# Two pairs of early loads merged into one transfer each, and gamma split in 8 pieces, in a streaming RMSNorm + GELU kernel

## The chip, the cores and the metric

The kernel runs on one core of one Trainium2 chip. The metric is the time of one execution on the device in microseconds (us). "Engines" without a name are compute engines (ACT is ScalarE, DVE is VectorE, POOL is GpSimd, SP is SyncE); the 16 engines that move data are always called DMA engines here. All runs named below gave correct results. All were in the normal ("fast") state, with one exception that is marked.

## The reference

For `x` of shape 8 x 1024 x 2048 (fp32, 67.1 MB) and `gamma` of 2048 values:

```python
rms = np.sqrt(np.mean(x ** 2, axis=-1, keepdims=True) + eps)
out = gamma * x / rms
return 0.5 * out * (1 + np.tanh(np.sqrt(2 / np.pi) * (out + 0.044715 * out ** 3)))
```

Every element is read once and written once, so 134.25 MB cross between HBM and SBUF. That is the work that the time is spent on.

## The kernel before

The 8192 rows are cut into 16 groups of 4 MB (128 partitions x 4 rows x 2048). Six slots in SBUF hold a group each. Loads are issued by SyncE and stores by ScalarE, so there are two DMA queues. In a pass over the groups ScalarE does the squares of group `g`, POOL makes the reciprocal root, DVE multiplies by gamma, and ScalarE then does the GELU of group `g - 1` and issues its store. The load that reuses the slot follows it.

```python
    slot = [sbuf.tile([P, R, D], FP32, name=f"slot{i}") for i in range(SLOTS)]
    ...
    store_pieces = {G - 1: [(0, 2), (2, 2)]}      # the last group is stored in two parts
    ...
    def load(g):
        nc.sync.dma_start(out=slot[g % SLOTS], in_=x3[g])
    ...
    def gelu_store(g):
        for r, n in store_pieces.get(g, [(0, R)]):
            ...                                    # GELU of the rows r .. r+n, in place
            nc.scalar.dma_start(
                out=o3[g, :, r : r + n, :], in_=slot[g % SLOTS][:, r : r + n, :]
            )
    ...
        for g in range(SLOTS):
            load(g)
        nc.scalar.dma_start(                       # gamma, in D // GW = 16 pieces
            out=gamma_row[:, :, 0:GW],
            in_=gamma.rearrange("(o a b) -> o a b", o=1, b=GW),
        )
        ...
        for g in range(G + 1):
            if g < G:
                squares(g)
                inverse_rms(g)
                scale(g)
            if g:
                gelu_store(g - 1)
                if g - 1 + SLOTS < G:
                    load(g - 1 + SLOTS)
```

Completion of a transfer is told by a semaphore; the transfers of the program take eight of them in turn. At the end SyncE waits for all of them, in a fixed order, before the program closes.

Of the kernel before, what the change touches and what calls it, by code (L numbers as in the profile page):

```python
# [1 line left out]

# [4 lines left out]

FP32 = mybir.dt.float32
ALU = mybir.AluOpType
ACT = mybir.ActivationFunctionType  # L10

P = 128
ROWS = 4
SLOTS = 6

GW = 128


@with_exitstack
def kernel(  # L20
    ctx: ExitStack,
    tc: tile.TileContext,
    x: bass.AP,
    gamma: bass.AP,
    eps: bass.AP,
    out: bass.AP,
):




    nc = tc.nc
    D = x.shape[-1]
    R = ROWS
    eps_f = float(eps)
    x3 = x.rearrange("b s d -> (b s) d").rearrange("(g p r) d -> g p r d", p=P, r=R)
    o3 = out.rearrange("b s d -> (b s) d").rearrange("(g p r) d -> g p r d", p=P, r=R)
    G = x3.shape[0]

    sbuf = ctx.enter_context(tc.tile_pool(name="sbuf", bufs=1))  # L40
    psum = ctx.enter_context(
        tc.tile_pool(name="psum", bufs=1, space=bass.MemoryType.PSUM)
    )
    slot = [sbuf.tile([P, R, D], FP32, name=f"slot{i}") for i in range(SLOTS)]
    gamma_row = sbuf.tile([1, D // GW, GW + 16], FP32, name="gamma_row")
    ones = sbuf.tile([1, P], FP32, name="ones")
    warm = sbuf.tile([1, 1], FP32, name="warm")
    power = sbuf.tile([P, R], FP32, name="power")
    ssq = sbuf.tile([P, G, R], FP32, name="ssq")
    rstd = sbuf.tile([P, G, R], FP32, name="rstd")  # L50
    ms = sbuf.tile([P, R], FP32, name="ms")
    y = sbuf.tile([P, R], FP32, name="y")
    z = sbuf.tile([P, R], FP32, name="z")
    gamma_ps = psum.tile([P, D], FP32, name="gamma_ps")
    junk = psum.tile([P, D], FP32, name="junk")

    store_pieces = {G - 1: [(0, 2), (2, 2)]}
    scale_pieces = {G - 1: [(0, 1), (1, 1), (2, 1), (3, 1)]}

    def load(g):  # L60
        nc.sync.dma_start(out=slot[g % SLOTS], in_=x3[g])  # L61

    def squares(g):
        for r in range(R):
            nc.scalar.activation(  # L65
                out=junk,
                in_=slot[g % SLOTS][:, r, :],
                func=ACT.Square,
                accum_out=ssq[:, g, r : r + 1],
            )  # L70

    def scale(g):
        for r, n in scale_pieces.get(g, [(0, R)]):
            rows = slot[g % SLOTS][:, r : r + n, :]
            nc.vector.tensor_tensor(  # L75
                out=rows,
                in0=rows,
                in1=gamma_ps.unsqueeze(1).to_broadcast([P, n, D]),
                op=ALU.mult,
            )  # L80

    def inverse_rms(g):

        v = nc.gpsimd
        v.tensor_scalar(  # L85
            out=ms, in0=ssq[:, g, :], scalar1=1.0 / D, scalar2=eps_f,
            op0=ALU.mult, op1=ALU.add,
        )
        v.tensor_tensor(out=y, in0=ms, in1=power, op=ALU.pow)  # L89
        v.tensor_tensor(out=z, in0=y, in1=y, op=ALU.mult)  # L90
        v.tensor_tensor(out=z, in0=z, in1=ms, op=ALU.mult)  # L91
        v.tensor_scalar(  # L92
            out=z, in0=z, scalar1=-0.5, scalar2=1.5, op0=ALU.mult, op1=ALU.add
        )
        v.tensor_tensor(out=rstd[:, g, :], in0=z, in1=y, op=ALU.mult)  # L95

    def gelu_store(g):
        for r, n in store_pieces.get(g, [(0, R)]):
            for q in range(r, r + n):
                row = slot[g % SLOTS][:, q, :]  # L100
                nc.scalar.activation(  # L101
                    out=row, in_=row, func=ACT.Gelu_apprx_tanh,
                    scale=rstd[:, g, q : q + 1],
                )
            nc.scalar.dma_start(  # L105
                out=o3[g, :, r : r + n, :], in_=slot[g % SLOTS][:, r : r + n, :]
            )

    with tc.manual_schedule():
        for g in range(SLOTS):  # L110
            load(g)
        nc.scalar.dma_start(
            out=gamma_row[:, :, 0:GW],
            in_=gamma.rearrange("(o a b) -> o a b", o=1, b=GW),
        )
        nc.gpsimd.memset(power, -0.5)  # L116
        nc.vector.memset(warm, 0.0)  # L117
        nc.vector.memset(ones, 1.0)  # L118
        nc.scalar.activation(out=warm, in_=warm, func=ACT.Gelu_apprx_tanh)  # L119
        for k in range(0, D, 512):  # L120
            nc.tensor.matmul(  # L121
                out=gamma_ps[:, k : k + 512],
                lhsT=ones,
                rhs=gamma_row[:, k // GW : (k + 512) // GW, 0:GW],
                start=True,
                stop=True,
# [12 lines that stand above are left out]
# [1 line left out]
_INS = ['x', 'gamma', 'eps']  # L140
_OUTS = [((8, 1024, 2048), 'float32')]

_NUMBERS = {'eps': 9.999999747378752e-06}


# [26 lines left out]
```

## Time and profile before

| | before |
|---|---|
| time, median of 3 executions | 317.47 us (317.44 to 317.48) |
| the execution that was profiled | 318.66 us, of which the profile's span is 316.9 |
| transfers | 16 loads, 17 stores, 1 for gamma: 34 |
| DMA share of the span, by queue | loads 49.5%, stores 49.1% |
| ACT, DVE, POOL busy | 79%, 44%, 10% |

The lines below are from the page of the kernel before: the span, the busy tenths of ScalarE and of the DMA engines in 40 equal slices of it, the packets, the two queues (packets, MB, share of 16 DMA engines' span; q1 is the queue of the loads, q10 that of the stores), and the issues (KB each, median us from issue to landing).

```profile
span 316.9 us, 473 instructions
ACT  1379999999999997959689595995959859599800
DMA  8999999999999999999999999999999999999995
DMA packets 4787, 134.25 MB, mean 424 GB/s; under 512 B 544, under 2 KB 560, under 8 KB 560
q1 hardware_dynamic: 2304, 67.11, 49.5%
q10 hardware_dynamic: 2480, 67.12, 49.1%
slot<-in_x_dram SPq DMA_DIRECT2D x16, 4096.0 KB, 37.1
out_dram<-slot ACTq DMA_DIRECT2D x15, 4096.0 KB, 38.6
out_dram<-slot ACTq DMA_DIRECT2D x2, 2048.0 KB, 15.0
```

The DMA engines are at 9 tenths or more in all slices but the first and the last, while ScalarE pauses. The DMA engines bound this kernel. Of the 4787 packets 544 are under 512 bytes: these are the 4-byte writes that raise the semaphores, 34 transfers x 16 DMA engines. The Trainium skill says the same of the mechanism (page "DMA: Bandwidth & Descriptors", section "Why a DMA increments its semaphore by 16 and not by 1"): each DMA engine that takes part ends with a write of its own to the semaphore. The page's section "Specifications" gives 435 GB/s as the ceiling; the trace agrees, as a 32 KB packet takes 1.213 us, which is 432 GB/s for 16 DMA engines.

What SyncE waited for at the end of the kernel before (us in total, times, longest us). L167 is the closing of the program.

```profile
SPq L167 <- DMA out_dram<-slot: 39.6, 1, 39.6
SPq L167 <- DMA slot<-in_x_dram: 36.6, 1, 36.6
```

One long wait is for a load and one is for the last store. The trace has the times of what follows the last landing at 315.88 us: SyncE still goes through three more waits, long fulfilled, at 315.94, 316.00 and 316.06, then closes at 316.12. The end of the span is at 316.88, 1.00 us after the landing.

### The profile page before, as it was taken

How to read it: one execution, taken by the hardware profiler on the slowest of the kernel's cores; microseconds unless marked ns; L12 is line 12 of the kernel's file. 1: busy time of each engine (PE TensorE's matmuls, PEld its weight loads, DVE VectorE, ACT ScalarE, POOL GpSimd, SP SyncE). 2: the span in 40 equal slices, each digit the busy share in tenths (PEclk: the TensorE clock that was granted, in tenths of full speed). 3: DMA queues.
4: the chain of work that ended last, by engine and by line, in shares of the span. 5: the costliest groups of instructions: out<-in, count | busy, mean ns of one | idle time of the engine just before them, and what ended most of it. 6: DMA issues, size and time to landing. Idle time of an engine off the chain costs nothing.

```text
span 316.9 us, 473 instructions
## 1 busy us (share of the span) xinstructions
PE 7.2 (2%) x8; PEld 2.5 (1%) x8; DVE 139.4 (44%) x21; ACT 251.1 (79%) x194; POOL 32.3 (10%) x101
## 2 busy tenths in 40 slices
PE   0900000000000000000000000000000000000000
PEld 0300000000000000000000000000000000000000
DVE  0038909090919191732808246091550905582000
ACT  1379999999999997959689595995959859599800
POOL 0020102020202020202002020020200102001000
DMA  8999999999999999999999999999999999999995
GB/s 328 414 451 426 434 393 459 401 459 402 459 405 455 426 434 431 430 434 426 438 426 455 410 455 418 443 426 430 434 430 435 422 459 405 459 414 447 422 420 230
DMA packets 4787, 134.25 MB, mean 424 GB/s; under 512 B 544, under 2 KB 560, under 8 KB 560
## 3 DMA queue, kind: packets, MB, share of 16 engines
q1 hardware_dynamic: 2304, 67.11, 49.5%
q10 hardware_dynamic: 2480, 67.12, 49.1%
q14 instruction: 3, 0.02, 0.0%
HBM read 67.12 MB, written 67.11 MB: 424 GB/s over the span
## 4 chain that ended last, share of the span: by engine, by line
DMA 56%; ACT 33%; issue 5%; ACTq 1%; SPq 0%
DMA slot<-in_x_dram 30%; DMA out_dram<-slot 26%; ACT slot L101 19%; ACT junk L65 14%; ACTq L105 1%; SPq L61 0%; ACTq L101 0%; ACTq L65 0%
## 5 line engine op out<-in xcount | busy, mean ns | idle before, releaser
L75 DVE TENSOR_TENSOR slot<-slot,gamma_ps 128x8192 f32<-128x8192 f32 (+1 forms) x19 | 139.2, 7340 | 147.0 <-ACT junk L65 147.0
L65 ACT ACTIVATE junk<-slot 128x2048 f32<-128x2048 f32 x64 | 120.4, 1881 | 47.3 <-DMA slot<-in_x_dram 43.7
L101 ACT ACTIVATE slot<-slot,rstd 128x2048 f32<-128x2048 f32 x64 | 122.8, 1989 | 0.9 <-ACT slot L101 0.9
L85 POOL TENSOR_SCALAR ms<-ssq 128x4 f32<-128x4 f32 x16 | 3.1, 194 | 247.5 <-ACT junk L65 247.5
L89 POOL TENSOR_TENSOR y<-ms,power 128x4 f32<-128x4 f32 x16 | 16.1, 1009 | 1.3
L65 ACT ACTIVATION_READ_ACCUMULATOR junk<-slot 128x1 f32 x64 | 12.0, 188 | 0.0
L121 PE MATMUL gamma_ps<-gamma_row,ones 1*128 1x512 f32 x8 | 7.2, 1072 | 8.4 <-DMA gamma_row<-in_gamma_dram 8.4
L95 POOL TENSOR_TENSOR rstd<-z,y 128x4 f32<-128x4 f32 x16 | 3.2, 201 | 1.3
L91 POOL TENSOR_TENSOR z<-z,ms 128x4 f32<-128x4 f32 x16 | 3.2, 201 | 1.3
L90 POOL TENSOR_TENSOR z<-y 128x4 f32<-128x4 f32 x16 | 3.2, 199 | 1.3
L92 POOL TENSOR_SCALAR z<-z 128x4 f32<-128x4 f32 x16 | 3.1, 194 | 1.4
L121 PEld LDWEIGHTS gamma_ps<-gamma_row,ones 1*128 1x128 f32 x8 | 2.5, 325 | 11.5 <-issue 11.5
L119 ACT ACT_TABLE_LOAD x1 | 1.3, 1283 | 1.3 <-PEq L153 1.3
L117 DVE MEMSET warm<- 1x1 f32 x1 | 0.1, 59 | 0.8 <-PEq L153 0.8
L119 ACT ACTIVATE warm<-warm 1x1 f32<-1x1 f32 x1 | 0.2, 202 | 0.0
L118 DVE MEMSET ones<- 1x128 f32 x1 | 0.2, 165 | 0.0
L116 POOL MEMSET power<- 128x4 f32 x1 | 0.1, 102 | 0.3 <-POOLq L153 0.3
L153 POOL MEMSET const-float32-0.0<- 128x1 f32 x1 | 0.1, 99 | 0.2 <-issue 0.2
L153 POOL MEMSET const-bfloat16-1.0<- 128x1 bf16 x1 | 0.1, 102 | 0.0
L153 POOL MEMSET const-uint8-127<- 128x1 uint8 x1 | 0.1, 102 | 0.0
L153 POOL MEMSET const-float32-1.0<- 128x1 f32 x1 | 0.1, 99 | 0.0
## 6 DMA issues: line engine op xcount, KB each, us to landing
slot<-in_x_dram SPq DMA_DIRECT2D x16, 4096.0 KB, 37.1
out_dram<-slot ACTq DMA_DIRECT2D x15, 4096.0 KB, 38.6
out_dram<-slot ACTq DMA_DIRECT2D x2, 2048.0 KB, 15.0
gamma_row<-in_gamma_dram ACTq DMA_DIRECT2D x1, 8.0 KB, 7.5
```

The lines of the kernel that those rows point to most:

```text
L65: nc.scalar.activation(out=junk, in_=slot[g % SLOTS][:, r, :], func=ACT.Square, accum_out=ssq[:, g, r : r + 1],)
L75: nc.vector.tensor_tensor(out=rows, in0=rows, in1=gamma_ps.unsqueeze(1).to_broadcast([P, n, D]), op=ALU.mult,)
L85: v.tensor_scalar(out=ms, in0=ssq[:, g, :], scalar1=1.0 / D, scalar2=eps_f, op0=ALU.mult, op1=ALU.add,)
L89: v.tensor_tensor(out=y, in0=ms, in1=power, op=ALU.pow)
L90: v.tensor_tensor(out=z, in0=y, in1=y, op=ALU.mult)
L91: v.tensor_tensor(out=z, in0=z, in1=ms, op=ALU.mult)
L92: v.tensor_scalar(out=z, in0=z, scalar1=-0.5, scalar2=1.5, op0=ALU.mult, op1=ALU.add)
L95: v.tensor_tensor(out=rstd[:, g, :], in0=z, in1=y, op=ALU.mult)
L101: nc.scalar.activation(out=row, in_=row, func=ACT.Gelu_apprx_tanh, scale=rstd[:, g, q : q + 1],)
L105: nc.scalar.dma_start(out=o3[g, :, r : r + n, :], in_=slot[g % SLOTS][:, r : r + n, :])
L119: nc.scalar.activation(out=warm, in_=warm, func=ACT.Gelu_apprx_tanh)
L121: nc.tensor.matmul(out=gamma_ps[:, k : k + 512], lhsT=ones, rhs=gamma_row[:, k // GW : (k + 512) // GW, 0:GW], start=True, stop=True,)
```

## The change

The intent is to remove those three waits from the end. With two transfers fewer, the last store gets another of the eight semaphores: the one that SyncE waits for last. So loads 2 and 3 become one transfer of 8 MB, and so do loads 4 and 5; for that, the six slots become parts of one tile. Gamma, which is read in pieces, is read in 8 pieces of 1 KB in place of 16 of 512 bytes.

```diff
-GW = 128
+GW = 256
+
+EARLY = [(0, 1), (1, 1), (2, 2), (4, 2)]
...
-    slot = [sbuf.tile([P, R, D], FP32, name=f"slot{i}") for i in range(SLOTS)]
+    ring = sbuf.tile([P, SLOTS, R, D], FP32, name="ring")
+    slot = [ring[:, i] for i in range(SLOTS)]
...
-    def load(g):
-        nc.sync.dma_start(out=slot[g % SLOTS], in_=x3[g])
+    def load(g, n=1):
+        i = g % SLOTS
+        nc.sync.dma_start(
+            out=ring[:, i : i + n], in_=x3[g : g + n].rearrange("g p r d -> p g r d")
+        )
...
-        for g in range(SLOTS):
-            load(g)
+        for g, n in EARLY:
+            load(g, n)
```

## The prediction

> **What bounds it now.** The 16 DMA engines. The profile's slices show DMA at 9 tenths or more in nearly every slice and a mean of 424 GB/s over the span; 2048 load packets and 1920 store packets of 32 KB take 1.21 us each, and all packets together take 312.2 us per engine of a 316.9 us span. That is at the 16-engine ceiling the Trainium skill gives ("DMA: Bandwidth & Descriptors", Specifications: about 435 GB/s). ACT is busy for 79%, DVE for 44%: both have slack. The trace begins moving data at 1.7 us; its last transfer lands at 315.88, its span ends at 316.88. In that last transfer 14 of 16 semaphore increments come by 313.83, the 15th at 314.89, the 16th at 315.88: two DMA engines lag.
>
> **What the change does.**
> 1. *End.* The semaphores of transfers rotate over eight. Before, the last store has number 1. SyncE ends with five wait instructions, over pairs (3,2), (4,1), (5,0), (6,PE), (7,ACT); the second one is released by the last store. Three more waits follow, one every 60 ns (315.94, 316.00, 316.06), then the drain at 316.12. With two transfers fewer (32 for 34), the last store gets number 7, the last of the five waits, so those three waits are over before. Saved: 3 x 60 ns = 0.18 us, all on the critical path, since nothing overlaps it. The rest of the closing barrier (0.75 us) stays.
> 2. *Two semaphore writes fewer per engine* (9 ns each in the packets) and gamma in 8 pieces instead of 16 (a 512-byte packet takes 27 ns; some engines lose one, others get one twice as long): under 0.05 us. Gamma is wanted by DVE at 21 us and its matmuls end at 15.5: off the path.
> 3. *Start.* Load 2 now lands with load 3 (42.2 us by the landings of before) and load 4 with load 5 (about 82). Before, the squares of group 2 began at 39.0, those of group 4 at 71.2. So ACT falls behind by about 3 us at group 2 and about 11 us at group 4: stores 1, 2 and 3 go out near 58, 74 and 98 us instead of 55, 71 and 87. The store queue holds 19.4 us of work per 4 MB store: store 2 ends at 102.7, so store 3 arrives 3 to 4 us before that, about as long as a store took from issue to its first packets (38.6 to 43.0). It may just run dry. ACT needs 16.1 us per group and the DMA 19.4, so 3.3 us per group are won back and by group 8 all is as before. Loads keep the engines busy in the meantime, so bytes are delayed, not lost. When the first store joined the loads, each engine had one packet about 0.5 us too long; if the store queue runs dry that may recur: up to +0.5 us, half likely.
> 4. *Which DMA engine ends last.* Its lag of 2 us over the others grew over the run (0.6 us spread at first, 3.4 at 259). Another order at the start may change it by up to 1 us either way. This is the largest uncertainty.
>
> **Prediction.** 317.47 - 0.18, with a little for step 3: 317.3 us, range 316.5 to 318.1. Faster by over 2%: 0.005; within 2%: 0.99; slower: 0.005.
>
> **Would show it right:** one wait instead of four between the last landing and the drain, and about 0.8 us from last landing to the end; ACT idle near 39 to 42 and 74 to 82 us; DMA still at 9 in all slices; total packet time unchanged.
>
> **Would show it wrong:** a slice near 100 us with DMA under 9; packets of the merged loads longer than 1.21 us; the last semaphore spread other than 2.6 us.

## More of the kernel before

The columns are the stretch and its length, the busy time of PE, PE's weight loads, DVE, ACT and POOL, the granted clock, the DMA share and GB/s.

```profile
180.00:200.00 20.00, 0.00 (x0) 0.00 (x0) 8.69 (x1) 16.24 (x14) 2.00 (x6) 1.00 1.01 434
200.00:220.00 20.00, 0.00 (x0) 0.00 (x0) 8.69 (x1) 16.21 (x15) 2.00 (x6) 1.00 1.00 433
220.00:240.00 20.00, 0.00 (x0) 0.00 (x0) 8.69 (x1) 16.22 (x13) 2.00 (x6) 1.00 1.00 431
240.00:260.00 20.00, 0.00 (x0) 0.00 (x0) 8.69 (x1) 15.52 (x13) 2.00 (x6) 1.00 1.00 433
```

The DMA share is 1.00 or 1.01 (a packet counts whole in the stretch in which it starts, so both columns vary a little), and 431 to 434 GB/s are moved.

## The result

| | before | after |
|---|---|---|
| time, median, same chip and rounds | 317.46 us (317.27 to 317.48, 4 executions) | 321.66 us (321.18 to 322.03, 4 executions) |
| span of the profile | 316.9 us | 319.4 us |
| last landing to the end of the span | 1.00 us | 0.84 us |

The ratio is 1.0133 (95%: 1.0115 to 1.0150). A ratio here is always the mean time of one kernel's fast runs over that of the other's of the same rounds, so not quite the ratio of the medians quoted. The kernel became 1.3% slower: under the 2% that would be called slower, but 3.6 us beyond the upper end of the predicted range. All outputs are right.

The page of the kernel after, the same lines:

```profile
span 319.4 us, 475 instructions
ACT  1379879992899999999999794985949859599800
DMA  8999999999999999999999999999999999999995
DMA packets 4739, 134.25 MB, mean 420 GB/s; under 512 B 504, under 2 KB 512, under 8 KB 512
q1 hardware_dynamic: 2272, 67.11, 49.9%
q10 hardware_dynamic: 2464, 67.12, 48.8%
out_dram<-ring ACTq DMA_DIRECT2D x15, 4096.0 KB, 34.7
ring<-in_x_dram SPq DMA_DIRECT2D x12, 4096.0 KB, 35.0
ring<-in_x_dram SPq DMA_DIRECT2D x2, 8192.0 KB, 59.5
```

The DMA line is the same to the digit. There are fewer packets (48 fewer), the same bytes, and yet the mean fell from 424 to 420 GB/s. The queues show where: q1 took 49.5% of 316.9 us, which is 156.9 us for each DMA engine, and now 49.9% of 319.4, which is 159.4: 2.5 us more. q10 took 155.6 and takes 155.9. The load packets became slower as a whole, though their number and size are the same; the store packets hardly did. The count of small packets agrees with the skill's rule for the number of DMA engines (same page, section "Why a DMA increments its semaphore by 16 and not by 1": at most 16, and such that it divides the slowest dimension): gamma in 8 pieces runs on 8 of them, and 31 x 16 + 8 is 504.

The windows view of the kernel after, the same stretches and columns:

```profile
180.00:200.00 20.00, 0.00 (x0) 0.00 (x0) 8.69 (x1) 15.66 (x13) 1.99 (x6) 1.00 1.00 421
200.00:220.00 20.00, 0.00 (x0) 0.00 (x0) 8.69 (x1) 15.68 (x13) 1.99 (x6) 1.00 1.01 426
220.00:240.00 20.00, 0.00 (x0) 0.00 (x0) 8.69 (x1) 15.88 (x13) 1.99 (x6) 1.00 1.00 423
240.00:260.00 20.00, 0.00 (x0) 0.00 (x0) 8.69 (x1) 15.51 (x13) 1.99 (x6) 1.00 0.99 418
```

The DMA share is still 0.99 to 1.01, at 418 to 426 GB/s for the 431 to 434 of before. So this is no idle time: it is busy time that moves less, 100 us and more after the merged loads have landed. These four stretches are the clearest: over the six stretches from 60 to 180 us the mean is 431 GB/s (before: 434).

The prediction's other steps hold. What SyncE waited for at the end, kernel after (L173 is the closing here):

```profile
SPq L173 <- DMA out_dram<-ring: 74.5, 5, 45.6
```

The last store's semaphore is now the last of the five. The trace has one wait after the last landing at 318.57 (at 318.584), and the closing at 318.65. From landing to closing that is 0.08 us for 0.24 before, and from landing to end 0.84 us are left of 1.00: 0.16 us were saved, where 0.18 were predicted. And the timeline of ScalarE in the kernel after (start us, us taken, instruction; in brackets the idle time before it and what ended it; cut to the store issues and the two long pauses):

```profile
38.37 0.36 ACTq L111 DMA_DIRECT2D out_dram<-ring  x1
...
42.19 1.88 ACT L71 ACTIVATE junk<-ring 128x2048 f32<-128x2048 f32 x1 [3.84 <-DMA ring<-in_x_dram]
...
57.89 0.34 ACTq L111 DMA_DIRECT2D out_dram<-ring  x1
...
73.97 0.34 ACTq L111 DMA_DIRECT2D out_dram<-ring  x1
...
80.76 1.88 ACT L71 ACTIVATE junk<-ring 128x2048 f32<-128x2048 f32 x1 [6.82 <-DMA ring<-in_x_dram]
...
96.46 0.34 ACTq L111 DMA_DIRECT2D out_dram<-ring  x1
```

Stores 1, 2 and 3 go out at 57.9, 74.0 and 96.5 us, where 58, 74 and 98 were predicted (before: 54.7, 70.8, 86.9). Store 3 is issued 5.3 us before store 2 lands (101.8, median over the DMA engines), so the store queue never ran dry.

### What the packets show

The trace records each packet with its start, duration, size and queue, but not its DMA engine. Chaining each packet to one that ends where it starts gives 16 chains, one for each DMA engine; a 4-byte write now and then falls into a neighbour's chain. Here is one chain of before and one of after around the first boundary between two stores. `L` is a load packet and `S` a store packet of 32 KB, with the start in us and the duration in ns; `L*` and `S*` are the semaphore writes that end a transfer on this DMA engine.

```
before  S@57.61:1213 L@58.82:1213 S@60.03:1213 L*@61.24:9 L@61.24:1213 S@62.45:1213 L@63.65:1213
        (its S*, at 61.24 too, stands in a neighbour's chain, which has two)
after   S@57.64:1213 L@58.85:1213 S@60.06:1213 L@61.27:1213 S*@62.48:9 L@62.48:1213 S@63.70:1213
```

Each DMA engine takes one packet of each queue in turn. That is what the Trainium skill says (page "DMA: Bandwidth & Descriptors", section "Queues, rings and completion order": a DMA engine goes round between its queues packet by packet, and SP and ACT own one ring each on all 16). A transfer of 4 MB is 8 packets and one semaphore write on each DMA engine. The chains show a thing that these sections leave out: **the semaphore write takes a turn of its own.** It lasts 9 ns, but in the kernel after, where the store queue spends its turn on `S*`, two load packets follow each other. Before, load and store boundaries coincide, both queues spend a turn on a semaphore write in the same round, and nothing shifts. The merged load of groups 4 and 5 has no semaphore write in its middle (at about 61 us). There the loads get ahead by one round, which is one load and one store packet, 2 x 1.213 = 2.43 us. And there they stay for the rest of the run:

| landing of, median of 16 DMA engines, us | in the middle of the run | store later than load by |
|---|---|---|
| before: loads | 100.4, 120.0, 139.3, 158.7 | |
| before: stores | 100.7, 120.2, 139.6, 158.9 | 0.2 |
| after: loads | 99.4, 118.9, 138.4, 158.0 | |
| after: stores | 101.8, 121.3, 140.8, 160.4 | 2.4 |

I call the last column the offset. At this offset of one round load packets become slow near the boundaries. One chain of after, and one of a later experiment (e13) in which the offset is three rounds:

```
after  L@174.22:1213 L@175.42:1213 L*@176.63:9 S@176.64:1371 L@178.01:1213 S*@179.22:9 S*@179.23:9
       L@179.24:1213 S@180.44:1213 L@181.65:1401 S@183.07:1220 L@184.28:1213
after  S@174.21:1213 S@175.43:1213 S@176.63:1213 L*@177.84:9 S@177.84:1213 L@179.05:1213 S*@180.26:9
       L@180.27:1934 S@182.20:1213 L@183.41:1215
e13    L*@174.01:9 S@174.01:1213 L@175.22:1213 S@176.43:1213 L@177.64:1213 S@178.85:1213 L@180.06:1213
       S*@181.27:9 L@181.28:1213 S@182.49:1213 L@183.70:1213
```

Counted over all chains: load packets longer than 1.3 us that start between 100 and 270 us are 9 before and 145 after. What all load packets take beyond 1.213 us, summed and divided by 16, is 1.51 us before (nearly all at the start, and near 41 us where the stores begin) and 4.15 us after: +2.64 us for each DMA engine, which is the +2.5 us of the queue line. While the merged loads themselves were in flight their packets were not slow.

For the traced execution of after (321.18) against the median one of before (317.47), 3.7 us are to be explained. The last store lands, on the median DMA engine, at 313.76 before and 316.49 after: +2.7 us, the slow load packets. The last DMA engine lags the median by 2.1 us in both traces; but the traced execution of before was itself 1.2 us over the median, and kernels that run at 317.4 (e6, e14) show a lag of only 0.8 to 0.9 us. So about +1.2 us is lag, an inference, as a median execution of before was not traced. The end gives -0.16.

In the trace of before, at least, the lag is no separate cause. One of the 16 chains has two stores and then two loads in a row at every boundary from 59.9 us on: this one DMA engine stands at the offset of one round, while the other 15 do not. It has 7 of the 9 slow load packets, and its load packets take 3.7 us beyond 1.213 each in sum, where those of the other chains take 1.0 to 2.0. That is about 2.3 us more than the middle chain (0.9 of it where the stores begin, 1.4 later), and the lag is 2.1. The traces of e6 and e14, at 317.4, have 2 slow load packets each. So the effect is seen inside one execution too, with 15 DMA engines as the comparison. What puts a single DMA engine there is not known.

### The profile page after: what moved, and what is told of

Its sections match the earlier page's. It is cut to its first block, busy times and chain, and to the rows that moved or that the text cites. A ratio compares the mean times of both kernels' runs of the same rounds, so it can differ in the third digit from the quotient of the medians.

```text
span 319.4 us, 475 instructions
## 1 busy us (share of the span) xinstructions
PE 7.2 (2%) x8; PEld 2.5 (1%) x8; DVE 139.4 (44%) x21; ACT 251.0 (79%) x194; POOL 32.1 (10%) x101
## 3 DMA queue, kind: packets, MB, share of 16 engines
q1 hardware_dynamic: 2272, 67.11, 49.9%
## 4 chain that ended last, share of the span: by engine, by line
DMA 60%; ACT 28%; issue 4%; another core or an unknown queue 2%; ACTq 1%; SPq 0%
DMA ring<-in_x_dram 35%; DMA out_dram<-ring 25%; ACT ring L107 17%; ACT junk L71 12%; ACTq L111 1%; SPq L65 0%; ACTq L107 0%
## 5 line engine op out<-in xcount | busy, mean ns | idle before, releaser
L81 DVE TENSOR_TENSOR ring<-ring,gamma_ps 128x8192 f32<-128x8192 f32 (+1 forms) x19 | 139.2, 7338 | 149.0 <-ACT junk L71 149.0
L71 ACT ACTIVATE junk<-ring 128x2048 f32<-128x2048 f32 x64 | 120.4, 1881 | 48.8 <-DMA ring<-in_x_dram 44.8
L107 ACT ACTIVATE ring<-ring,rstd 128x2048 f32<-128x2048 f32 x64 | 122.7, 1986 | 0.9 <-ACT ring L107 0.9
L71 ACT ACTIVATION_READ_ACCUMULATOR junk<-ring 128x1 f32 x64 | 11.9, 186 | 0.0
```

The costliest lines, as they stand in the source:

```text
L71: nc.scalar.activation(out=junk, in_=slot[g % SLOTS][:, r, :], func=ACT.Square, accum_out=ssq[:, g, r : r + 1],)
L81: nc.vector.tensor_tensor(out=rows, in0=rows, in1=gamma_ps.unsqueeze(1).to_broadcast([P, n, D]), op=ALU.mult,)
L107: nc.scalar.activation(out=row, in_=row, func=ACT.Gelu_apprx_tanh, scale=rstd[:, g, q : q + 1],)
```

## The experiments

Kernels of one batch ran on the same chip beside the kernel before. The batches are e1 to e4, e5 to e8, e9 to e12, e13 to e16, e17 and e18; the kernel before had medians of 317.43, 317.76, 317.39, 317.46 and 317.51 us in them.

The theories were: (offset) the missing turn of the load queue sets loads and stores apart, and the packets are slow because of that; (late) ScalarE's late groups 2 and 4, with late stores, are the cause; (merged) the 8 MB transfers, or the single tile, are the cause by themselves; (gamma) the 8 pieces are. All kernels are summed up in one table after the runs.

### e1: no merging, but the ring and gamma in 8 pieces

```diff
 (from after)
-EARLY = [(0, 1), (1, 1), (2, 2), (4, 2)]
+EARLY = [(0, 1), (1, 1), (2, 1), (3, 1), (4, 1), (5, 1)]
```

> The changed kernel without its merged loads: one ring tile and gamma in 8 pieces stay, six loads of 4 MB at the start. Theory 1 (turns: on each DMA engine the load queue and the store queue take turns packet by packet, and the 4-byte semaphore write that ends a transfer takes a whole turn; one load semaphore fewer while stores run puts the loads one packet ahead, so the ends of loads and stores no longer fall together, and the load packets beside a store's lone semaphore are slow): 317.4 us as before, excess of load packets over 1.21 us as before (1.6 us per DMA engine in the run). Theory 2 (ACT and so the stores are late): 317.4. Theory 3 (the new addresses of the ring, or gamma's share on 8 DMA engines, disturb the streams): 320 or more.

Measured: 318.52 us (317.27 to 319.13), ratio 1.0029 (1.0004 to 1.0055). Offset 0.2, 10 slow packets. The ring and gamma are not the main cause, though about 1 us stays with them.

### e2: only loads 2 and 3 merged; e3: only loads 4 and 5 merged

```diff
 (e2, from after; new line only)
+EARLY = [(0, 1), (1, 1), (2, 2), (4, 1), (5, 1)]
 (e3, from after; new line only)
+EARLY = [(0, 1), (1, 1), (2, 1), (3, 1), (4, 2)]
```

> Only loads 2 and 3 are one transfer (both end before the first store packet). Theory 1 (turns): no load semaphore is lost while stores run, so the ends of loads and stores stay together (medians within 0.3 us): 317.2 to 317.6. Theory 2 (late ACT): ACT is 3 us late for groups 2 to 4, so a part of the loss, 318 to 319. Theory 3 (a merged transfer is itself slow): half of the loss, 319 to 320.

> Only loads 4 and 5 are one transfer. Theory 1 (turns): one load semaphore is lost while stores run, loads end about 2.4 us before stores from then on: the whole loss, 321 to 322. Theory 2 (late ACT): most of the loss, about 320 to 321. Theory 3 (a merged transfer is itself slow): half, 319 to 320.

Measured: e2 319.21 us, ratio 1.0044 (1.0019 to 1.0069), offset 0.2, 24 slow packets. e3 321.98 us, ratio 1.0134 (1.0117 to 1.0151), offset 2.4, 139 slow packets. The merging of 4 and 5 carries it all; that of 2 and 3 does not, although it also is an 8 MB transfer. Turns tell them apart: the missing semaphore write of loads 2 and 3 falls at about 32 us, before any store runs (the first starts near 43 us), so there is no alternation to upset.

### e4 and e5: no merging, ScalarE made late on purpose

```diff
 (from before; e5. e4 had the same five squares, reading slot[g - 2])
             if g < G:
+                for r in range({2: 2, 4: 3}.get(g, 0)):
+                    nc.scalar.activation(
+                        out=junk, in_=slot[g][:, r, :], func=ACT.Square
+                    )
                 squares(g)
```

> The kernel before, with ACT made late by five extra squares with no use (two ahead of group 2, three ahead of group 4): stores 1, 2 and 3 go out near 58.8, 74.9 and 97.1 us, as in the changed kernel. No load is merged. Theory 1 (turns): 317.4 to 317.7, excess of load packets as before. Theory 2 (late ACT): 321 to 322, the whole loss.

> The run e4 waited for another group's load by mistake and is void for its question; this one repeats squares of the group that is next anyway. The kernel before, five extra squares without use on ACT (two ahead of group 2, three ahead of group 4): stores 1, 2, 3 near 58.8, 74.9 and 97 us, as in the changed kernel, no load merged. Theory 1 (turns): ends of loads and stores stay within 0.3 us of each other, 317.3 to 317.8. Theory 2 (late ACT): 320 to 322.

e4 was a mistake: the slot that its extra squares read had a new load under way, so they waited for it, ScalarE was late by some 60 us, and the DMA queues ran dry (372.3 us). It says nothing here. e5 puts stores 1, 2 and 3 at 58.6, 74.7 and 96.5 us, where the kernel after has 57.9, 74.0 and 96.5. Its four executions were 317.73, 321.05, 317.42 and 320.62 us, ratio 1.0038 (0.9979 to 1.0097). The traced one (317.73) has offset 0.3 and 9 slow packets. So lateness is not enough: two of four executions are as fast as before. But two are 3 us slower, and no trace of these exists. What they did stays open.

### e6 and e7: a tiny transfer added to one queue of the kernel before

A transfer of 64 bytes costs each DMA engine two turns of its queue (4 bytes of data, and the semaphore write), and next to no time. It is issued on ScalarE's queue after store 0 (e6), or on SyncE's before load 6 (e7).

```diff
 (e6, from before; e7 has nc.sync)
+    tiny = sbuf.tile([16, 1], FP32, name="tiny")
...
                 gelu_store(g - 1)
+                if g == 1:
+                    nc.scalar.dma_start(
+                        out=tiny, in_=gamma.rearrange("(a b) -> a b", a=16)[:, 0:1]
+                    )
```

> The kernel before with a transfer of 64 bytes without use (16 floats, one for each DMA engine) issued on ACT's queue right after store 0. Theory 1 (turns): its packet and its semaphore take two turns from the stores; counting turns, loads end 4 packets (4.9 us) ahead of stores from then on, and 64 bytes cost 2 us or more: 319.5 to 323. Theories 2 and 3: nothing is late or merged: 317.4.

> The kernel before with the same 64 bytes on SyncE's queue between loads 5 and 6. Theory 1 (turns): the loads lose two turns and end 2 packets (2.4 us) after the stores, the offset of the changed kernel with the other sign; every store's semaphore is again alone: 319 to 322 if only being apart counts, 317.4 if only loads ahead are harmful. Theories 2 and 3: 317.4.

Measured: e6 317.66 us, ratio 0.9990 (0.9966 to 1.0014), offset 4.9, 2 slow packets. e7 319.19 us, ratio 1.0041 (1.0012 to 1.0070), offset -2.5; between 80 and 100 us its packets took 1.1 us more than 1.213 each in sum, once, for each DMA engine (0.75 the loads, 0.36 the stores), and nearly nothing after. This supports one half of the theory and refutes the other as I first held it. Turns do set the offset, to the packet, with hardly a byte moved. But an offset as such costs nothing: at 4.9 us e6 has the speed of before. It must be the size of the offset.

### e8: the tiny transfer on SyncE's queue of the kernel after

```diff
 (from after, as e7)
+                    nc.sync.dma_start(
+                        out=tiny, in_=gamma.rearrange("(a b) -> a b", a=16)[:, 0:1]
+                    )
```

> The changed kernel with the same 64 bytes on SyncE's queue ahead of load 6. Theory 1 (turns): the loads lose two turns, which brings the ends of loads and stores together again (within 0.3 us): most of the loss comes back, 317.2 to 318.5, by adding a transfer. Theories 2 and 3: merged loads and late ACT stay, 321.5.

Measured: 342.8, 340.8, 343.46 and 317.19 us; the profiled one (342.8) counts as slow state, and no ratio is given. In that trace four of the 16 DMA engines (a fifth later) fall out of step with the rest from about 81 us on. Their slow store packets take about 1.85 us, and their last load lands at 297 to 300 us, some 20 us after that of the others. The one fast execution fits the theory, but one untraced time is not evidence. Unsettled.

### e9 and e10: a store in two halves, which adds one turn to the store queue

```diff
 (e9, from before, with g == 0; e10, from after, with g == 1)
-            nc.scalar.dma_start(
-                out=o3[g, :, r : r + n, :], in_=slot[g % SLOTS][:, r : r + n, :]
-            )
+            for p in range(0, P, P // 2) if g == 0 else [0]:
+                q = p + (P // 2 if g == 0 else P)
+                nc.scalar.dma_start(
+                    out=o3[g, p:q, r : r + n, :],
+                    in_=slot[g % SLOTS][p:q, r : r + n, :],
+                )
```

> So far: merging 4 and 5 alone costs the whole loss (e3), but loads ending 4.9 us ahead of stores (e6) cost nothing. So theory 1 in its first form is wrong: being apart is not enough. Theory 1b: it is the offset of two packets (2.4 us, loads ahead) that is bad, however it comes about. Here, in the kernel before, store 0 is two transfers of 64 partitions each: one more store semaphore, one turn less for the stores, nothing merged, nothing late. Counting turns: loads end 2.4 us ahead of stores. Theory 1b: 320.5 to 322.5 with load packets over 1.3 us at each later boundary. Theory 4 (the loss needs the merged transfer itself, or what it does to ACT, on top of the offset): 317.3 to 318.

> The changed kernel, with store 1 as two transfers of 64 partitions: one more turn lost by the stores, so loads end 4 packets (4.9 us) ahead, as in e6, instead of 2. Merged loads and late ACT stay. Theory 1b: 317.3 to 318.5. Theory 4: 321 to 322.5.

Measured: e9 324.83 us, ratio 1.0232 (1.0198 to 1.0265), offset 2.4, 136 slow packets. e10 319.15 us, ratio 1.0057 (1.0028 to 1.0086), offset 4.8, 2 slow packets. This pair is the strongest evidence. Without any merged load, without the ring, without late groups and with gamma as before, one added store turn brings the kernel before to the offset of one round, and the slow packets appear. The queue lines of e9, from its page:

```profile
span 323.6 us, 474 instructions
DMA packets 4803, 134.25 MB, mean 415 GB/s; under 512 B 560, under 2 KB 576, under 8 KB 576
q1 hardware_dynamic: 2304, 67.11, 50.1%
q10 hardware_dynamic: 2496, 67.12, 48.5%
```

Of 323.6 us, 50.1% is 162.1 us for the load queue: 5.2 more than before. Only part of it recurs: between 40 and 70 us, while the halves were in flight, packets of both queues took some 2.7 us more than in before (1.6 the loads, 1.1 the stores), once: a cost of the split itself. The remainder returns near the boundaries, mostly at every other one, 0.6 to 0.7 us each time. e10 is the counterpart. It adds a further turn to the kernel after, moves the offset from one round to two, and removes the slow packets (145 become 2), at a one-time cost of about 1.4 us.

### e11 and e12: a load in two halves, which gives the load queue its turn back

```diff
 (e12, from before; e11, from after)
-                    load(g - 1 + SLOTS)
+                    if g == 1:
+                        for p in (0, 64):
+                            nc.sync.dma_start(
+                                out=slot[0][p : p + 64], in_=x3[SLOTS][p : p + 64]
+                            )
+                    else:
+                        load(g - 1 + SLOTS)
```

> The changed kernel, with load 6 as two transfers of 64 partitions: the load queue has its lost turn back and, counting turns, loads and stores end together again from load 6 on. Theory 1b: 317.2 to 318.5. Theory 4: 321 to 322.5. As in e8, which has the same offset but a turn order that differs between DMA engines, some executions may fall into a state of 340.

> The kernel before, with load 6 as two transfers of 64 partitions: a control of the split itself. Counting turns, loads lose one turn; loads and stores still end together, in the other order. Theory 1b: 317.3 to 318.0. If splitting as such is costly, or any change of the turn order is: over 319.

Measured: e11 325.36 us, ratio 1.0242 (1.0216 to 1.0268); e12, the control, 325.47, ratio 1.0246 (1.0219 to 1.0274). The times cannot tell anything, as the split load has a large cost of its own: nearly all its packets take 1.6 to 2.7 us, with a median of 2.07, in place of 1.213 (e12), and loads and stores together lost about 6 us for each DMA engine in e11 and 8 in e12, once, before 110 us. The traces can: after 110 us e12 has 2 slow load packets, and e11 has 8. In e11 the DMA engines did not agree any more (offset 1.0 on the median), so it is a weak test.

### e13: the tiny transfer on ScalarE's queue of the kernel after

The edit of e6, on the kernel after. It takes the offset from one round to three and leaves everything else of the change in place: merged loads, late groups, gamma in 8 pieces.

> The changed kernel with the 64 bytes of e6 on ACT's queue after store 0: counting turns, loads end 6 packets (7.3 us) ahead of stores. Merged loads, ring and late ACT stay as in the changed kernel. Theory 1b (two packets is the bad offset): no load packets over 1.3 us at the boundaries after 100 us, and 317.3 to 318.5, from one transfer more. Theory 4 (the merged transfer does it): 321 to 322.5.

Measured: 317.76 us (317.42 to 317.94), ratio 0.9999 (0.9981 to 1.0017), offset 7.3, 2 slow packets. Its page:

```profile
span 315.9 us, 479 instructions
DMA packets 4771, 134.25 MB, mean 425 GB/s; under 512 B 536, under 2 KB 544, under 8 KB 544
q1 hardware_dynamic: 2272, 67.11, 49.7%
q10 hardware_dynamic: 2496, 67.12, 49.2%
tiny<-in_gamma_dram ACTq DMA_DIRECT2D x1, 0.1 KB, 28.7
```

It adds a transfer and 32 packets of 4 bytes to the kernel after, and 4 us are gone. 49.7% of 315.9 us is 157.0 us for the load queue, as before the change (156.9). Merged loads, the ring and late ScalarE groups are thereby cleared of the recurring cost: they are all here.

### e14, e15: the ring alone, and gamma in 8 pieces alone

```diff
 (e14, from after)                                (e15, from before)
-GW = 256                                         -GW = 128
+GW = 128                                         +GW = 256
-EARLY = [(0, 1), (1, 1), (2, 2), (4, 2)]
+EARLY = [(0, 1), (1, 1), (2, 1), (3, 1), (4, 1), (5, 1)]
```

> The kernel before with one ring tile for the six slots, and nothing else. e1 (ring and gamma in 8 pieces) had 317.27 to 319.13. If the ring's addresses matter: about 318.3. If not: 317.4.

> The kernel before with gamma in 8 pieces, and nothing else. If gamma's share on 8 DMA engines is what moved e1: about 318.3. If not: 317.4.

Measured, with 6 executions each: e14 317.41 us, ratio 0.9992 (0.9976 to 1.0007); e15 318.88 us, ratio 1.0039 (1.0022 to 1.0056). Of the 1 us of e1 the ring has nothing, and gamma's pieces have it. In the trace of e15 the median DMA engine lands its last store at 314.08 us and the last one at 315.88. In e14 these are 313.77 and 314.62. So most of it is the lag of the DMA engines that end last. The traces tell more if one counts, at each boundary from 60 to 260 us, the DMA engines whose store lands over 1.5 us after the middle one of the loads, which marks the offset of one round. In the traces at 0 turns these are none in e14, 1 in before (the one found above), 1 in e5 from 100 us on, 2 in e15 and in e16, 2 and then 3 in e1, and 4 in e2. Their traced executions took 317.41, 318.66, 317.73, 318.65, 318.78, 318.99 and 319.27 us. So the loss with gamma's 8 pieces looks like the same effect on a few DMA engines, though one trace of each kernel does not prove it. Why 8 packets for gamma at the start should put DMA engines there is open: e16, with 16 pieces, has two as well, and e13, with 8 pieces, shows no loss.

### e16: the kernel before with its last store whole and gamma on POOL's queue

```diff
 (from before)
-    store_pieces = {G - 1: [(0, 2), (2, 2)]}
+    store_pieces = {}
...
-        nc.scalar.dma_start(
+        nc.gpsimd.dma_start(
             out=gamma_row[:, :, 0:GW],
```

> An attempt at the change's aim without its loss: the kernel before with the last store in one transfer and gamma issued from GpSimd's queue. That too leaves 32 transfers on the two queues and gives the last store semaphore 7, and no load semaphore is lost while stores run. Three waits of 60 ns fewer at the end: 317.2 to 317.3 if nothing else moves; up to 1 us either way if the DMA engine that ends last changes.

Measured: 317.90 us (317.32 to 318.78, 6 executions), ratio 1.0006 (0.9987 to 1.0026). The end is the short one (last landing 316.10, one wait at 316.11, closing at 316.18): another way to the change's aim, with 32 transfers on the two queues and no merging. The gain from landing to end (0.91 us for 1.00) is lost in the spread of 1.5 us between executions.

### e17 and e18: the change without its gamma part, and a version without the cost

e17 is the kernel after with gamma in 16 pieces. e18 is e17 with the tiny transfer of e13, and with the last group stored whole, so that again 32 transfers are made and the last store's semaphore is the last one awaited.

```diff
 (from after; e17 has the first edit only)
-GW = 256
+GW = 128
...
+    tiny = sbuf.tile([16, 1], FP32, name="tiny")
...
-    store_pieces = {G - 1: [(0, 2), (2, 2)]}
+    store_pieces = {}
...
                 gelu_store(g - 1)
+                if g == 1:
+                    nc.scalar.dma_start(
+                        out=tiny, in_=gamma.rearrange("(a b) -> a b", a=16)[:, 0:1]
+                    )
```

> The changed kernel with gamma back in 16 pieces; the merged loads and the offset of two packets stay. e15 had 1.4 us for gamma's 8 pieces alone, e13 (8 pieces, offset of six packets) only 0.3. If the two parts add up: about 320.3, with slow load packets at the boundaries as in the changed kernel. If the offset is all of it here: 321.7.

> The changed kernel put right: merged loads as they are, the 64 bytes on ACT's queue (offset of six packets), gamma in 16 pieces, the last store whole, so that 32 transfers give it semaphore 7. No slow load packets, one wait between the last landing and the drain (0.18 us saved), the last DMA engine about 0.9 us behind the median as in e13 and e14: 317.0 to 317.4, against 317.4 to 317.5 for the kernel before.

Measured: e17 321.12 us (320.75 to 321.65), ratio 1.0110 (1.0092 to 1.0128), offset 2.4, 127 slow packets. The offset alone carries most of the loss; its interval overlaps that of the full change, so what gamma's pieces add to it is not told. e18: 317.19 us (317.10 to 317.51, 5 executions), ratio 0.9988 (0.9974 to 1.0003), offset 7.3, 2 slow packets. The windows view of e18, columns as above:

```profile
180.00:200.00 20.00, 0.00 (x0) 0.00 (x0) 8.69 (x1) 16.25 (x13) 1.99 (x6) 1.00 1.01 434
200.00:220.00 20.00, 0.00 (x0) 0.00 (x0) 8.69 (x1) 16.19 (x15) 1.99 (x6) 1.00 1.00 433
220.00:240.00 20.00, 0.00 (x0) 0.00 (x0) 8.69 (x1) 16.23 (x13) 1.99 (x6) 1.00 1.00 431
240.00:260.00 20.00, 0.00 (x0) 0.00 (x0) 8.69 (x1) 15.57 (x13) 1.99 (x6) 1.00 1.01 437
```

It is back at 431 to 437 GB/s in all four stretches (before: 431 to 434). It has the lowest median of all, but its interval holds 1.000, so it is not shown to beat the kernel before.

### All runs by the turns that one queue has more than the other

"Turns" counts, while both queues run, the turns that the store queue spends more than the load queue, each of about 10 ns: semaphore writes and the 4-byte data of the tiny transfer. Each turn should move the loads ahead by one round of 2.43 us. (A lead of the stores reads as one round less: at -1 the store's semaphore write comes right before the load's, with nothing in between.) The measured offset is the median between 140 and 260 us.

| turns | kernel | offset, us | slow load packets, 100 to 270 us | median, us |
|---|---|---|---|---|
| -2 | e7 | -2.5 | 4 | 319.19 |
| -1 | e12 | -0.2 | 39, of them 38 before 140 us (split load) | 325.47 |
| 0 | before | 0.2 | 9 | 317.46 |
| 0 | e14, e5 (traced one), e1 | 0.2, 0.3, 0.2 | 2, 9, 10 | 317.41, 317.73, 318.52 |
| 0 | e15, e16, e2 | 0.2, 0.2, 0.2 | 12, 15, 24 | 318.88, 317.90, 319.21 |
| 0 | e11 (split load, DMA engines disagree) | 1.0 | 35, of them 28 before 140 us | 325.36 |
| **+1** | **after** | **2.4** | **145** | **321.66** |
| **+1** | **e3** | **2.4** | **139** | **321.98** |
| **+1** | **e17** | **2.4** | **127** | **321.12** |
| **+1** | **e9 (split store)** | **2.4** | **136** | **324.83** |
| +2 | e6, e10 | 4.9, 4.8 | 2, 2 | 317.66, 319.15 |
| +3 | e13, e18 | 7.3, 7.3 | 2, 2 | 317.76, 317.19 |

e4 and e8 are left out for the reasons given. The offsets follow the count of turns throughout, with e11 the one in doubt. Of the kernels in the table, the four at +1 are exactly those that have over 100 slow packets. (e4 has 123 too, all before 230 us, in the part of the run in which its queues ran dry and filled again. So this offset is not the only way to slow load packets.)

## Why the prediction was wrong, point by point

1. *The bound.* Right: the DMA engines, at the ceiling. This should have warned that any slowing of packets is paid in full.
2. *The end.* Right: 0.18 us predicted, 0.16 read from the traces, with one wait in place of four after the last landing.
3. *"Two semaphore writes fewer per engine (9 ns each in the packets)", under 0.05 us.* This is the step that failed. It priced the semaphore write by its duration. The runs showed that it is a turn in an alternation. One turn less on the load queue while stores run shifts loads and stores by 2.43 us for the rest of the run (after, e3), and at that offset the load packets near the boundaries are slow: +2.6 us for each DMA engine. Taking the offset away and leaving the rest gives the time back (e13); making the offset in the kernel before makes the slow packets (e9).
4. *"Loads keep the engines busy in the meantime, so bytes are delayed, not lost", and "total packet time unchanged".* The second part was wrong: the time of the load packets grew from 156.9 to 159.4 us for each DMA engine. The first is true, and was no reason for it: busy time can move fewer bytes.
5. *The late groups.* The times were right (57.9, 74.0, 96.5 us for 58, 74, 98), the store queue did not run dry, and the +0.5 us for that did not come. e13 has nearly the same lateness (58.3, 74.4, 93.5) without loss. Lateness is not needed either (e9). Whether it has a part in the two slow executions of e5 is open.
6. *Gamma.* Off the critical path as said, yet under 0.05 us was wrong: 8 pieces alone cost 1.4 us (e15, against 317.46), mostly in the DMA engines that end last. In its trace two DMA engines stand at the offset of one round; how the pieces put them there is open.
7. *Which DMA engine ends last, 1 us either way.* The size was about right, but by luck, as the reason was not seen: it accounts for an inferred 1.2 us, and in the trace of before the lag comes from the slow packets of one DMA engine, not from an order of its own. And I took the lag of 2.1 us in the trace of before as typical. The profiled execution was 318.66 us where the median was 317.47; that difference was in the data given and should have been subtracted first.
8. *The signs named as telling.* "Packets of the merged loads longer than 1.21 us" looked at the wrong ones: the slow packets belong to the loads that came after. "DMA still at 9 in all slices" held and tells nothing of this. GB/s by stretch, and the time of each queue, did.

What stays open: why load packets slow down at an offset of one round and not at zero, two or three. That they do is shown by four kernels against all the others in the table, and by one DMA engine against 15 in the trace of before; the cause inside the memory or the DMA engines is not seen in these traces. Open too are how gamma's pieces move single DMA engines to that offset, the slow executions of e5, and the state of e8.

## What to carry to other kernels

When two DMA queues saturate the same DMA engines, do not price a removed or added transfer by the duration of its small packets; count the turns that it takes from its queue, because they set for the rest of the run which packets of the two queues meet. Look at GB/s by stretch and at each queue's time, not only at the DMA share, which stays at 1.00 while packets take longer. And compare the execution in the trace with the median of the untraced ones before using its tail as the base of a prediction.

## What the Trainium skill lacked or had wrong

- Page "DMA: Bandwidth & Descriptors", sections "Queues, rings and completion order" and "Why a DMA increments its semaphore by 16 and not by 1": they state the alternation by packets and the final semaphore write, but not that this write of 9 ns uses a whole turn of its queue. The runs show offsets of 2.4, 4.9 and 7.3 us where the store queue spends one, two and three such turns more than the load queue.
- No page says that the relative position of load and store boundaries changes the time of packets. Four kernels at an offset of 2.4 us had 127 to 145 load packets over 1.3 us; the kernel before had 9. In the kernel after, the load packets took 2.6 us more for each DMA engine.
- Same page, "Rules for kernel authors", advises against two transfers to disjoint partition halves because "they serialize". The advice is right, but the cost here was more than that: the packets of the split load took 2.07 us (median) in place of 1.213, and the kernel before went from 317.39 to 325.47 us (e12).
- Same page, "Where 436 GB/s comes from", says that between HBM and SBUF the HBM side, about 358 GB/s for a core, binds. Taken alone, that sentence does not hold for these runs: this kernel, on one core, moved 424 GB/s over its whole span, reads and writes together, and 431 to 434 in steady state, so the figure of 435 is the one that bound. The same passage does call its own measurement of 425 GB/s near the fabric's rate; the sentence lacks its condition.
- No page says how far the DMA engines of one transfer end apart. At the end of these runs the last of 16 was 0.8 to 2.8 us behind the median one (0.8 in e6, 2.8 in e3), and the number of pieces of an 8 KB load at the start changed the kernel by 1.4 us (e15).
